# Low halves of the token projections' weights: from a negation and an accumulating DMA to one subtraction on VectorE

## The chip, the core and the metric

The kernel runs on one core of one Trainium2 chip. The metric is the device time of one execution in microseconds (us), as a median of runs; the profile is of one further execution. The engines are TensorE (PE in the profile), VectorE (DVE), ScalarE (ACT), GpSimd (POOL) and SyncE (SP).

## What is computed

One decoder layer on 512 tokens of width 1024, in float32:

```python
h = rms_norm(x, ln1_g)
z = h @ w_in                      # one input projection for all three branches and the gates
a = gelu(z_a); u, v = split(a)    # branch 0: chunked spatial gating
y_a = (u * chunked_spatial_gating(layer_norm(v), sg_w, sg_b)) @ w_a_out
c = p * sigmoid(g_lin)            # branch 1: convolution of 31 taps, layer norm, SiLU
c = silu(layer_norm(causal_depthwise_conv(c, cv_w, cv_b)))
y_b = c @ w_b_out
q, k = rms_norm(q), rms_norm(k)   # branch 2: stick-breaking attention, 8 heads of 64
y_c = stick_breaking_attention(q, k, vv) @ w_c_out
gates = sigmoid(z_g + b_gate)
x = x + (gates[0] * y_a + gates[1] * y_b + gates[2] * y_c) @ w_out
h2 = rms_norm(x, ln2_g)
up = causal_depthwise_conv(h2 @ w_up, ffn_conv_w, ffn_conv_b)   # width 3
x = x + (silu(gate) * val) @ w_down
```

## The kernel before

Every matrix product is made of three matmuls: each float32 operand is held as a high half (the value rounded to the matmul's format) and a low half (what the rounding left), and TensorE adds high times high, high times low and low times high in one PSUM bank (`mm3`, L124, L127 and L128; in the token projections L495 to L497). The activations' halves are made once. The weights come as 140 tiles of 128x1024, one after the other, and each is split on arrival by `wload`: SyncE loads the raw tile (two buffers, `wr`), ScalarE casts it to the high half `wh` (L173), and the low half `wl` follows. Six buffers hold three pairs of halves, so the halves of tile n can be written when TensorE is done with tile n-3. `wload` runs two tiles ahead of TensorE.

How the low half is made depends on the tile (`bydma`). For 120 of the tiles VectorE subtracts: raw minus high (L175; the first four tiles are split by other lines). For the 20 tiles of the token projections (the `NTOK` tiles 8 to 27: the two halves of branch 0, q, k and v) ScalarE writes minus the high half (L178) and GpSimd issues a DMA (L179) that reads the same weights from HBM once more and adds them into it.

In this text unit n is the work of TensorE on weight tile n, counted from 0: 24 matmuls of 512 columns, for full tiles. Units 0 to 7 are branch 1's input projection, 8 to 27 the token projections, then for each branch gates and outputs (branch 0: units 28 to 39, branch 1: 40 to 51 with its outputs in 44, 45, 50 and 51, branch 2: gates in 52 to 59 and outputs in 60 to 63), the output projection (64 to 71), the feed-forward's up (72 to 115) and down (116 to 139).

Between these units lies the side work of the branches, written as generators: `conv` (the 31 taps on VectorE, L363, in two pairs of channel blocks, and then the layer norm: two column sums by matmul with `onesW`, L314 and L315, the reciprocal root with ScalarE's Ln and Exp and VectorE's L320 and L134 to L136, then L397, a sigmoid on ScalarE, L402, L404 and a `split` into `cT`), `hi` (branch 0's norm and the norms of q and k), `soft` (turning q and k, L646; scores, L676 and L677; their sigmoids on ScalarE), `scan` (the cumulative products on VectorE, L723, and a multiply, L726), and `av` (turning the result, L736, splitting it, the matmuls with v, L749 and L750, into one PSUM bank whose contents L756 and L757 take out). The outputs' matmuls use two PSUM banks in turn, `mm`, which the gates' sigmoids on ScalarE or the multiply L827 on VectorE empty.

The order is a planner's. It keeps three clocks, for TensorE, VectorE and ScalarE, in modelled microseconds; `spend` moves them and `fill` lets side work be issued while the clock of the engine that it needs is behind TensorE's. Each half unit moves TensorE's clock by 2.72 (`PEU / 2`), and by `wspend` the two others by the split of the tile that is loaded next: for a tile with its low half by DMA, nothing on VectorE's clock and 1.04 on ScalarE's; for the others 0.61 and 0.52. Before a branch's outputs `finish` issues whatever is left of the side work that they need. The framework's scheduler then sets each engine's order from the order of issue, with the weights' splits, gates and evacuations first (`hot`), and every engine runs its own list in that order.

Of the kernel before, what the change touches and what calls it, by code (L numbers as in the profile page):

```python
# [11 lines left out]
AF = mybir.ActivationFunctionType  # L12
ALU = mybir.AluOpType
# [25 lines left out]
NZB, NTOK, NZG, NY, NOUT, NUP, NDN = 8, 20, 24, 12, 8, 44, 24  # L39
# [6 lines left out]
def tile_block(ctx: ExitStack, tc: tile.TileContext, xT, x0g, wall, cst, lnv, sgw, outT):  # L46
    nc = tc.nc
    act, dve, pool, pe, sp = nc.scalar, nc.vector, nc.gpsimd, nc.tensor, nc.sync
# [37 lines left out]
    f = lambda ap: ap.bitcast(F32)  # L86
# [16 lines left out]
    def load(out, in_):  # L103
        i = sp.dma_start(out=out, in_=in_)
        after(i, dlast[0])
        dlast[0] = i.ins
# [8 lines left out]
    def split(hi, lo, src):  # L115
        act.copy(out=hi, in_=src)  # L116
        dve.tensor_tensor(out=lo, in0=src, in1=f(hi), op=ALU.subtract)
# [5 lines left out]
    def mm3(out, ah, al, bh, bl, start, stop, behind=None):  # L123
        i = pe.matmul(out=out, lhsT=ah, rhs=bh, start=start, stop=False)  # L124
        after(i, behind)
        mark[0] = i.ins
        pe.matmul(out=out, lhsT=ah, rhs=bl, start=False, stop=False)  # L127
        pe.matmul(out=out, lhsT=al, rhs=bh, start=False, stop=stop)  # L128
# [9 lines left out]
    def hot():  # L138

        return tc.high_priority(int(HOT * tc.cur_priority))  # L140
# [9 lines left out]
    state = {"next": 0}  # L150
# [1 line left out]
    HOT = 0.7  # L152
    WARM = 7

    def bydma(i):

        return NZB <= i < NZB + NTOK

    def wspend():

        if bydma(state["next"]):
            spend(PEU / 2, 0, SPA)
        else:
            spend(PEU / 2, SPD / 2, SPA / 2)

    def wload(i):
        n = 768 if i >= NW - NDN and (i - (NW - NDN)) % 3 == 2 else 1024
        raw = wr.tile([P, 1024], F32, tag="wr", name="wr")
        hi = ws.tile([P, 1024], F32R, tag="w", name="wh")
        lo = ws.tile([P, 1024], F32R, tag="w", name="wl")  # L170
        load(raw[:, :n], wall[i, :, :n])
        with hot():
            act.copy(out=hi[:, :n], in_=raw[:, :n])  # L173
            if not bydma(i):
                dve.tensor_tensor(out=lo[:, :n], in0=raw[:, :n], in1=f(hi[:, :n]), op=ALU.subtract)  # L175
            else:

                act.activation(out=lo[:, :n], in_=f(hi[:, :n]), func=AF.Copy, scale=-1.0)  # L178
                pool.dma_start(out=lo[:, :n], in_=wall[i, :, :n], accum_op=ALU.add)  # L179
        wq[i] = (hi, lo)  # L180

    def wnext(i):
        while state["next"] < min(NW, i + 1 + AHEAD):
            wload(state["next"])
            state["next"] += 1
        return wq.pop(i)
# [6 lines left out]
    def spend(pe=0.0, dve=0.0, act=0.0):  # L193
        clk["pe"] += pe
        clk["dve"] += dve
        clk["act"] += act
# [14 lines left out]
    def fill():  # L211
        for k in ("dve", "act"):
            clk[k] = max(clk[k], clk["pe"] - 5.0)
        live = {n: bool(side[n]) for n in side}
        while True:
            for n, need in (("hi", ()), ("av", ()), ("scan", ()), ("conv", ("dve",)), ("soft", ("act", "dve"))):
                if live[n] and all(clk[k] < clk["pe"] for k in need):
                    live[n] = step(side[n])
                    break
            else:  # L220
                return
# [10 lines left out]
    def cd(n, s=0):  # L232
        return 0.15 + s * 0.06 + n * 0.001042
# [30 lines left out]
    for k in range(KD):  # L264
        i, j = k // 2, half[k % 2]
# [3 lines left out]
        raw, hi, lo = w4[i]  # L269
# [140 lines left out]
    def chan_unit(i, ps, xs):  # L410

        hi, lo = wnext(i)
        for k in range(KD):
            ks = slice(k * P, (k + 1) * P)
            mm3(ps, hi[:, ks], lo[:, ks], xs[k][0], xs[k][1], k == 0, k == KD - 1)
            if k == 3:
                wspend()
                fill()
        wspend()

    def group4():
        return [MM(), MM(), Z(), AV()]
# [1 line left out]
    PEU, SPD, SPA = 5.44, cd(1024), ca(1024)  # L424
# [4 lines left out]
    for kk in range(4):  # L429
        hi, lo = wnext(iw)  # L430
# [3 lines left out]
        for j in range(2):  # L434
# [6 lines left out]
            if k == 0:  # L441
# [4 lines left out]
                for c, a, b in order:  # L446
                    i = pe.matmul(out=g[c], lhsT=a[:, c * P:(c + 1) * P], rhs=xg[k][b],
                                  start=a is hi and b == 0, stop=False)
# [32 lines left out]
    def tok_group(evac, dve_c, act_c):  # L481
        nonlocal iw
        g = group4()
        for kk in range(4):
            hi, lo = wnext(iw)
            iw += 1

            order = [(c, j) for c in range(4) for j in range(2)] if kk == 3 else \
                [(c, j) for j in range(2) for c in range(4)]
            for n, (c, j) in enumerate(order):  # L490
                k = 2 * kk + j
                js = slice(j * 512, (j + 1) * 512)
                cs = slice(c * P, (c + 1) * P)
                xh, xl = xn[k][0][:, cs], xn[k][1][:, cs]
                pe.matmul(out=g[c], lhsT=xh, rhs=hi[:, js], start=k == 0, stop=False)  # L495
                pe.matmul(out=g[c], lhsT=xh, rhs=lo[:, js], start=False, stop=False)  # L496
                mark[0] = pe.matmul(out=g[c], lhsT=xl, rhs=hi[:, js], start=False, stop=k == KD - 1).ins  # L497
                if k == KD - 1:
                    with hot():
                        evac(c, g[c])  # L500
                if n == 3 or n == 7:
                    if n == 7 and kk == 3:
                        spend(0, dve_c, act_c)
                    wspend()
                    fill()


# [306 lines left out]
    def outputs(gate, src, first, last):  # L814
        nonlocal iw
        ocs = sorted(gate)
        for i2 in range(len(ocs) // 2):
            hi, lo = wnext(iw)
            iw += 1
            for jj in range(2):  # L820
                oc = ocs[2 * i2 + jj]
                ps = MM()
                for k in range(KW):
                    ks = slice((jj * KW + k) * P, (jj * KW + k + 1) * P)
                    mm3(ps, hi[:, ks], lo[:, ks], src[k][0], src[k][1], k == 0, k == KW - 1)
                with hot():
                    dve.tensor_tensor(out=gate[oc], in0=ps, in1=gate[oc], op=ALU.mult)  # L827
                if first:
                    m[oc] = gate[oc]
                else:  # L830
                    dve.tensor_tensor(out=m[oc], in0=m[oc], in1=gate[oc], op=ALU.add)
                if last:
                    mg[oc] = PR()
                    split(mg[oc][0], mg[oc][1], m[oc])
                wspend()
                spend(0, 2 * cd(T), 0)
                fill()

# [14 lines left out]
    for oc in range(KD):  # L853
        x1[oc] = S()
        sp.dma_start(out=x1[oc], in_=xT[oc])
        hi, lo = wnext(iw)
# [18 lines left out]
    for fch in range(KF):  # L875
        cv = []
        pss = []
        for gv in range(2):
            hi, lo = wnext(iw)
# [8 lines left out]
        for gv in range(2):  # L888
# [6 lines left out]
            for s in (1, 2):  # L895
                dve.scalar_tensor_tensor(out=a[:, :T - s], in0=t[:, s:T], scalar=c_("fw", ch * 3 + s),  # L896
                                         in1=a[:, :T - s], op0=ALU.mult, op1=ALU.add)
# [12 lines left out]
    for oc in range(KD):  # L910
        ps = Z()
        for k in range(KF):
            if k % 8 == 0:
                hi, lo = wnext(iw)
# [104 lines left out]
```

## Time and profile before

| | us |
|---|---|
| median of 3 runs | 804.87 (804.74 to 805.3) |
| the profiled execution's own time | 804.76 |
| its span, from the first to the last instruction | 802.9 |
| TensorE busy in the span | 796.2 |
| VectorE busy | 547.4 |
| ScalarE busy | 384.2 |

What lies around the span of the profiled execution is 804.76 - 802.9 = 1.86 us. A matmul's record overlaps with the next one's, so the busy time of TensorE says only that it is hardly ever without work; how fast it goes is read from the starts of its matmuls. DMA moved 90.96 MB at a mean of 113 GB/s, 10.49 MB of it through the queue of GpSimd's accumulating DMAs.

### The profile page before, as it was taken

The numbers are of one execution on the slowest core, as the hardware profiler recorded it, in microseconds if no ns is written. First come the engines' busy times: TensorE is split into PE (matmuls) and PEld (weight loads), VectorE is DVE, ScalarE is ACT, GpSimd is POOL, SyncE is SP. The second block draws the span as 40 slices with busy tenths as digits, with TensorE's granted clock in tenths as the row PEclk, the third lists the DMA queues.
The fourth block names the chain that finished last, engine by engine and source line by source line (L and its number), as shares of the span: only waits on it lengthen the run. The fifth ranks groups of instructions, "written<-read, shape, count | busy, mean of one in ns | idle before, by whom it ended". The sixth has DMA issues, their size and how long they took to land.

```text
span 802.9 us, 9339 instructions
## 1 busy us (share of the span) xinstructions
PE 796.2 (99%) x3607; PEld 660.4 (82%) x3607; DVE 547.4 (68%) x752; ACT 384.2 (48%) x546; POOL 44.4 (6%) x65
## 2 busy tenths in 40 slices
PE   9999999999999999999999999999999999999998
PEld 7888888887888888788888888888888888888886
DVE  7779988887797888633855777777777777322221
ACT  7476555446967486333344544444444444211110
POOL 0012111000112022000000000000000000000000
PEclk9999999999999999999999999999999999999999
DMA  7389886632231212222343322322322322333230
GB/s 270 106 226 211 186 197 153 154 106 80 80 104 57 75 53 79 78 81 104 113 140 141 105 81 103 105 92 93 105 97 87 105 104 77 109 105 134 102 105 26
DMA packets 27692, 90.96 MB, mean 113 GB/s; under 512 B 3072, under 2 KB 3712, under 8 KB 27648
## 3 DMA queue, kind: packets, MB, share of 16 engines
q1 hardware_dynamic: 24624, 79.76, 29.2%
q0 software_dynamic: 2880, 10.49, 7.8%
q8 instruction: 28, 0.46, 0.2%
q14 instruction: 16, 0.13, 0.1%
q10 hardware_dynamic: 144, 0.13, 0.0%
HBM read 88.27 MB, written 2.10 MB: 113 GB/s over the span
## 4 chain that ended last, share of the span: by engine, by line
PE 96%; ACT 1%; DVE 1%; DMA 1%; issue 0%; SPq 0%; DVEq 0%; ACTq 0%
PE z L124 18%; PE z L127 18%; PE z L128 18%; PE mm L124 8%; PE mm L128 8%; PE mm L127 8%; PE mm L496 2%; PE mm L497 2%; PE mm L495 2%; PE a L497 1%; PE z L497 1%; PE a L496 1%; PE z L496 1%; PE a L495 1%; PE z L495 1%; PE z L736 1%
## 5 line engine op out<-in xcount | busy, mean ns | idle before, releaser
L173 ACT CAST wh<-wr 128x1024 fp32r<-128x1024 f32 (+1 forms) x136 | 141.7, 1042 | 227.1 <-PE z L127 113.5
L124 PE MATMUL z<-s,wh 128*128 128x512 f32 x599 | 233.0, 389 | 0.0
L128 PE MATMUL z<-s,wl 128*128 128x512 f32 x599 | 233.0, 389 | 0.0
L127 PE MATMUL z<-s,wh 128*128 128x512 f32 x599 | 233.0, 389 | 0.0
L175 DVE TENSOR_TENSOR wl<-wr,wh 128x1024 fp32r<-128x1024 f32 (+1 forms) x116 | 140.2, 1209 | 107.9 <-ACT wh L173 106.5
L128 PEld LDWEIGHTS z<-s,wl 128*128 128x128 f32 x599 | 112.4, 188 | 23.4
L124 PEld LDWEIGHTS z<-s,wh 128*128 128x128 f32 x599 | 112.4, 188 | 23.4
L127 PEld LDWEIGHTS z<-s,wh 128*128 128x128 f32 x599 | 112.4, 188 | 23.3
L124 PE MATMUL mm<-s,wh 128*128 128x512 f32 x302 | 120.4, 399 | 0.5 <-ACT s L113 0.4
L127 PE MATMUL mm<-s,wh 128*128 128x512 f32 x302 | 117.6, 389 | 0.0
L128 PE MATMUL mm<-s,wl 128*128 128x512 f32 x302 | 117.3, 391 | 0.0
L363 DVE SCALAR_TENSOR_TENSOR s<-s,cst 128x511 f32<-128x511 f32 (+29 forms) x120 | 80.2, 732 | 0.0
L128 PEld LDWEIGHTS mm<-s,wl 128*128 128x128 f32 x302 | 56.7, 188 | 12.4
L896 DVE SCALAR_TENSOR_TENSOR h<-h,cst 128x511 f32<-128x511 f32 x88 | 65.7, 748 | 1.5
L124 PEld LDWEIGHTS mm<-s,wh 128*128 128x128 f32 x302 | 56.8, 188 | 12.1 <-ACT s L113 1.0
L127 PEld LDWEIGHTS mm<-s,wh 128*128 128x128 f32 x302 | 56.8, 188 | 10.7
L893 DVE TENSOR_TENSOR h<-z,rs 128x512 f32<-128x512 f32 x44 | 30.2, 687 | 39.8 <-PE z L128 39.8
L894 ACT ACTIVATE h<-h,cst 128x512 f32<-128x512 f32 x44 | 35.9, 816 | 3.2 <-DVE h L893 3.0
L116 ACT CAST s<-h 128x512 fp32r<-128x512 f32 x18 | 11.2, 620 | 49.1 <-DVE h L901 49.1
L113 ACT ACTIVATE h<-h 128x512 f32<-128x512 f32 x22 | 13.9, 632 | 41.9 <-DVE h L896 41.9
L495 PE MATMUL mm<-wh,s 128*128 128x512 f32 x80 | 31.2, 390 | 0.0
L496 PE MATMUL mm<-wl,s 128*128 128x512 f32 x80 | 31.1, 389 | 0.0
(184 smaller groups left out, 901.0 us busy)
## 6 DMA issues: line engine op xcount, KB each, us to landing
wr<-wall SPq DMA_DIRECT2D x128, 512.0 KB, 3.3
wl<-wall POOLq DMA_DIRECT2D x20, 512.0 KB, 5.5
s<-xT SPq DMA_DIRECT2D x15, 256.0 KB, 4.1
wr<-wall SPq DMA_DIRECT2D x8, 384.0 KB, 3.1
outT<-s SPq DMA_DIRECT2D x7, 256.0 KB, 2.0
h<-wall SPq DMA_DIRECT2D x3, 512.0 KB, 6.9
s<-sgw SPq DMA_DIRECT2D x2, 256.0 KB, 4.3
s<-lnv SPq DMA_DIRECT2D x2, 256.0 KB, 5.5
```

The costliest lines, as they stand in the source:

```text
L124: i = pe.matmul(out=out, lhsT=ah, rhs=bh, start=start, stop=False)
L127: pe.matmul(out=out, lhsT=ah, rhs=bl, start=False, stop=False)
L128: pe.matmul(out=out, lhsT=al, rhs=bh, start=False, stop=stop)
L173: act.copy(out=hi[:, :n], in_=raw[:, :n])
L175: dve.tensor_tensor(out=lo[:, :n], in0=raw[:, :n], in1=f(hi[:, :n]), op=ALU.subtract)
L363: after(dve.scalar_tensor_tensor(out=acc[j][:, :T - s], in0=cc[j][:, s:], scalar=c_("cvw", j * TAPS + s), in1=acc[j][:, :T - s], op0=ALU.m ...
L495: pe.matmul(out=g[c], lhsT=xh, rhs=hi[:, js], start=k == 0, stop=False)
L496: pe.matmul(out=g[c], lhsT=xh, rhs=lo[:, js], start=False, stop=False)
L497: mark[0] = pe.matmul(out=g[c], lhsT=xl, rhs=hi[:, js], start=False, stop=k == KD - 1).ins
L893: dve.tensor_tensor(out=t[:, :T], in0=pss[gv], in1=rs2, op=ALU.mult)
L894: act.activation(out=a, in_=t[:, :T], func=AF.Identity, scale=c_("fw", ch * 3), bias=c_("fb", ch))
L896: dve.scalar_tensor_tensor(out=a[:, :T - s], in0=t[:, s:T], scalar=c_("fw", ch * 3 + s), in1=a[:, :T - s], op0=ALU.mult, op1=ALU.add)
```

## The change

All tiles are split in the one way: `wload` calls `split`, which casts on ScalarE (now L116) and subtracts on VectorE (now L117). `bydma` is gone, and with it `wspend`: each half unit now moves the planner's clocks by the same amounts for all tiles, so for each of the 20 tiles VectorE's clock moves by 1.22 more and ScalarE's by 1.04 less than before. In the changed file all later lines have numbers that are smaller by 17 (L363 is L346, L827 is L810, and so on).

```diff
--- before.py
+++ after.py
@@ -152,17 +152,6 @@
     HOT = 0.7
     WARM = 7
 
-    def bydma(i):
-
-        return NZB <= i < NZB + NTOK
-
-    def wspend():
-
-        if bydma(state["next"]):
-            spend(PEU / 2, 0, SPA)
-        else:
-            spend(PEU / 2, SPD / 2, SPA / 2)
-
     def wload(i):
         n = 768 if i >= NW - NDN and (i - (NW - NDN)) % 3 == 2 else 1024
         raw = wr.tile([P, 1024], F32, tag="wr", name="wr")
@@ -170,13 +159,7 @@
         lo = ws.tile([P, 1024], F32R, tag="w", name="wl")
         load(raw[:, :n], wall[i, :, :n])
         with hot():
-            act.copy(out=hi[:, :n], in_=raw[:, :n])
-            if not bydma(i):
-                dve.tensor_tensor(out=lo[:, :n], in0=raw[:, :n], in1=f(hi[:, :n]), op=ALU.subtract)
-            else:
-
-                act.activation(out=lo[:, :n], in_=f(hi[:, :n]), func=AF.Copy, scale=-1.0)
-                pool.dma_start(out=lo[:, :n], in_=wall[i, :, :n], accum_op=ALU.add)
+            split(hi[:, :n], lo[:, :n], raw[:, :n])
         wq[i] = (hi, lo)
 
     def wnext(i):
@@ -414,9 +397,9 @@
             ks = slice(k * P, (k + 1) * P)
             mm3(ps, hi[:, ks], lo[:, ks], xs[k][0], xs[k][1], k == 0, k == KD - 1)
             if k == 3:
-                wspend()
+                spend(PEU / 2, SPD / 2, SPA / 2)
                 fill()
-        wspend()
+        spend(PEU / 2, SPD / 2, SPA / 2)
 
     def group4():
         return [MM(), MM(), Z(), AV()]
@@ -501,7 +484,7 @@
                 if n == 3 or n == 7:
                     if n == 7 and kk == 3:
                         spend(0, dve_c, act_c)
-                    wspend()
+                    spend(PEU / 2, SPD / 2, SPA / 2)
                     fill()
 
 
@@ -832,7 +815,7 @@
                 if last:
                     mg[oc] = PR()
                     split(mg[oc][0], mg[oc][1], m[oc])
-                wspend()
+                spend(PEU / 2, SPD / 2, SPA / 2)
                 spend(0, 2 * cd(T), 0)
                 fill()
```

The planner and the scheduler make another order of this. On VectorE, in the token projections: before, the taps of the convolution (`s<-s,cst`) and branch 0's norm stand there without a weight's split between them.

```order
L117 TENSOR_TENSOR s<-s 128x512
L535 BN_AGGR mv<-st 128x2
L534 BN_STATS st<-b 128x6 x2
L535 BN_AGGR mv<-st 128x2
L363 SCALAR_TENSOR_TENSOR s<-s,cst 128x495
L535 BN_AGGR mv<-st 128x2
L534 BN_STATS st<-b 128x6
```

With the change the same norm's statistics stand seven taps of each channel block earlier (after the first tap of 503 columns, not after the last of 496), and a low half stands after every 2 to 13 instructions:

```order
L518 BN_AGGR mv<-st 128x2
L529 SCALAR_TENSOR_TENSOR b<-b,mv,s 128x512
L346 SCALAR_TENSOR_TENSOR s<-s,cst 128x501 x2
L346 SCALAR_TENSOR_TENSOR s<-s,cst 128x500
L523 TENSOR_SCALAR v_890<-mv 128x4
L529 SCALAR_TENSOR_TENSOR b<-b,mv,s 128x512
L346 SCALAR_TENSOR_TENSOR s<-s,cst 128x500
L117 TENSOR_TENSOR wl<-wr,wh 128x1024
L346 SCALAR_TENSOR_TENSOR s<-s,cst 128x499 x2
```

So the taps as a whole have moved to later units. On TensorE the first 31 units are in the same order as before; after them the side work has moved. The layer norm's column sums stood in units 31 and 34 and now stand in 39 and 42; head 0's scores in unit 34, now behind unit 43; the last attention matmul in unit 54, now in unit 60. Where branch 1's outputs begin (unit 44, banks `mm_2148` and `mm_2163`; `s_2084`, `s_2091`, `s_2117` and the numbers one above are the high and low halves of `cT`) TensorE now has this, with nothing else of the units between it and the second column sum but the rest of unit 42 and unit 43:

```order
L660 MATMUL z_2192<-s_1879,s_1877 128x128
L629 MATMUL z_2203<-ident_204,s_1012 128x128
L629 MATMUL z_2203<-ident_204,s_1020 128x128
L124 MATMUL mm_2148<-s_2084,wh_2033 128x512
L629 MATMUL z_2203<-ident_204,s_1031 128x128
...
L127 MATMUL mm_2148<-s_2085,wh_2033 128x512
L128 MATMUL mm_2148<-s_2084,wl_2034 128x512
L124 MATMUL mm_2148<-s_2091,wh_2033 128x512
L127 MATMUL mm_2148<-s_2092,wh_2033 128x512
```

Between the second matmul of that column sum and this first output stand 46 matmuls; in the order of before 294 stand between them. On VectorE the end of that norm now stands like this (`s_2085`, `s_2092`, `s_2118` and `s_2139` are the four low halves of `cT`; `h_2179` is head 0's scan, `wl_2144` the low half of unit 46, and L810 empties the bank of unit 44's first product):

```order
L387 TENSOR_TENSOR s_575<-s_575,s_1933 128x512
L117 TENSOR_TENSOR wl_2144<-wr_2142,wh_2143 128x1024
L117 TENSOR_TENSOR s_2085<-s_575,s_2084 128x512
...
L117 TENSOR_TENSOR s_2118<-s_1284,s_2117 128x512
L385 TENSOR_SCALAR s_1286<-s_1286,cst_85 128x512
L387 TENSOR_TENSOR s_1286<-s_1286,s_1991 128x512
L706 SCALAR_TENSOR_TENSOR h_2179<-h_2179,s_862 128x512
L117 TENSOR_TENSOR s_2139<-s_1286,s_2138 128x512
L706 SCALAR_TENSOR_TENSOR h_2179<-h_2179,s_862 128x384
L706 SCALAR_TENSOR_TENSOR h_2179<-h_2179,s_862 128x256
L810 TENSOR_TENSOR s_1988<-mm_2148,s_1988 128x512
```

Before, the same norm's end stood among branch 0's outputs, and its last low half, too, had other work around it:

```order
L402 TENSOR_SCALAR s_980<-s_980,cst_85 128x512
L117 TENSOR_TENSOR s_2047<-s_978,s_2046 128x512
L757 TENSOR_TENSOR s_2072<-a_2008,s_2072 64x512
L404 TENSOR_TENSOR s_980<-s_980,s_1744 128x512
L827 TENSOR_TENSOR s_1922<-mm_2082,s_1922 128x512
L175 TENSOR_TENSOR wl_2098<-wr_2096,wh_2097 128x1024
L117 TENSOR_TENSOR s_2079<-s_980,s_2078 128x512
L827 TENSOR_TENSOR s_1973<-mm_2102,s_1973 128x512
```

## Rows read from the trace of the kernel before

**Rows 1.** The page: engines' busy time, share of the span, instructions; granted clock by slices.

```profile
span 802.9 us, 9339 instructions
...
PE 796.2 (99%) x3607; PEld 660.4 (82%) x3607; DVE 547.4 (68%) x752; ACT 384.2 (48%) x546; POOL 44.4 (6%) x65
...
PEclk9999999999999999999999999999999999999999
```

**Rows 2.** Busy time by stretches, whole core.

```profile
core 0: us, PE busy (x) PEld busy (x) DVE busy (x) ACT busy (x) POOL busy (x), PEclk, DMA share, GB/s
...
60.00:80.00 20.00, 20.00 (x90) 16.57 (x89) 20.00 (x34) 13.13 (x16) 4.78 (x6) 1.00 0.92 210
```

**Rows 3.** Waits, TensorE alone: who waited for whom, total, times, longest.

```profile
PE z L247 <- POOL ident masks.py:197: 1.3, 1, 1.3
...
PE mm L124 <- ACT s L113: 0.4, 1, 0.4
```

**Rows 4.** Timeline of TensorE, first gates of branch 0: start, length.

```profile
163.26 0.39 PE L124 MATMUL mm<-s,wh 128*128 128x512 f32 x1
...
168.71 0.39 PE L124 MATMUL mm<-s,wh 128*128 128x512 f32 x1
```

**Rows 5.** Groups by form, VectorE.

```profile
L175 DVE TENSOR_TENSOR wl<-wr,wh 128x1024 fp32r<-128x1024 f32 x108 | 132.6, 1227 | 107.9 <-ACT wh L173 106.5
...
L723 DVE TENSOR_TENSOR_SCAN h<-h,s 128x512 f32<-128x512 f32 x8 | 9.9, 1236 | 4.6 <-ACT h L113 4.3
...
L402 DVE TENSOR_SCALAR s<-s,cst 128x512 f32<-128x512 f32 x4 | 2.2, 541 | 0.1
```

**Rows 6.** Groups by form, ScalarE.

```profile
L173 ACT CAST wh<-wr 128x1024 fp32r<-128x1024 f32 x128 | 134.9, 1054 | 205.0 <-PE z L127 91.4 <-PE a L496 40.9 <-PE mm L127 36.1
...
L178 ACT ACTIVATE wl<-wh 128x1024 fp32r<-128x1024 f32 x20 | 21.2, 1059 | 0.3
...
L113 ACT ACTIVATE s<-s 128x512 f32<-128x512 f32 x8 | 5.0, 629 | 7.7 <-DVE s L320 4.5 <-DVE s L348 3.2
...
L113 ACT ACTIVATE s<-s,cst 128x512 f32<-128x512 f32 x4 | 3.2, 830 | 0.0
```

**Rows 7.** DMA issues: size, median us from issue to landing.

```profile
wl<-wall POOLq DMA_DIRECT2D x20, 512.0 KB, 5.5
```

**Rows 8.** Timeline of VectorE, second norm of the convolution branch.

```profile
217.07 0.69 DVE L136 SCALAR_TENSOR_TENSOR s<-s 128x512 f32<-128x512 f32 x1
217.79 1.29 DVE L397 TENSOR_TENSOR s<-s 128x512 f32<-128x512 f32 x2
...
220.67 1.22 DVE L175 TENSOR_TENSOR wl<-wr,wh 128x1024 fp32r<-128x1024 f32 x1
221.80 0.42 DVE L117 TENSOR_TENSOR s<-z,s 128x256 fp32r<-128x256 f32 x1
...
231.69 0.67 DVE L404 TENSOR_TENSOR s<-s 128x512 f32<-128x512 f32 x1
```

**Rows 9.** Timeline of TensorE: that norm's sum, last attention matmul, branch 2's outputs.

```profile
205.83 0.40 PE L315 MATMUL z<-s,onesW 128*128 128x512 f32 x1
...
265.98 0.52 PE L736 MATMUL z<-ident,h 128*128 128x128 f32 x3
266.25 0.47 PE L124 MATMUL mm<-s,wh 128*128 128x512 f32 x1
...
344.04 0.28 PE L750 MATMUL a<-s,b 128*128 128x128 f32 x1
...
374.14 0.39 PE L124 MATMUL mm<-s,wh 128*128 128x512 f32 x1
```

**Rows 10.** Timeline of TensorE at its longest wait in the middle.

```profile
325.40 0.39 PE L128 MATMUL mm<-s,wl 128*128 128x512 f32 x1
326.77 0.47 PE L749 MATMUL a<-s,b 128*128 128x512 f32 x1 [0.98 <-DVE s L757]
```

**Rows 11.** Groups, TensorE: the seven warm-up matmuls.

```profile
L247 PE MATMUL z<-s 128*128 128x512 f32 x7 | 3.3, 651 | 1.3 <-POOL ident masks.py:197 1.3
```

## The prediction

> **What bounds the kernel now.** I read the page first. TensorE is busy 796.2 of 802.9 us, and the granted clock reads nine tenths or more in every slice [rows 1]. Then the stretches: in 60 to 80 us VectorE is busy all 20.00 us and DMA shows its highest share, 0.92, and TensorE still makes 90 matmuls at a granted clock of 1.00, its 2.4 GHz level [rows 2]. Then the pace. Unit 28 starts at 163.26 and unit 29 at 168.71 [rows 4]: 24 matmuls in 5.45 us, 0.227 us each. So the time of this kernel is the number of matmuls times 0.227 us plus the waits of TensorE, and the waits are small: 1.3 us at the start, 0.4 for a gate [rows 3], and one of 326.77 - 325.40 - 0.23 = 1.14 us where a matmul waits for VectorE to empty the attention's bank [rows 10]. The change leaves the matmuls as they are. It can win at most the last two, about 1.5 us, and it loses whatever new waits it makes for TensorE. A load on another engine costs nothing until TensorE stands still for it, and so I look for places where it would.
>
> **What the change removes.** Twenty negations on ScalarE at 1.059 us, 21.2 us [rows 6], and twenty transfers of 512 KB, each 5.5 us from issue to landing [rows 7]. TensorE waits for none of them in the trace, so their removal is worth 0. Their cover is the two units by which weights are split ahead.
>
> **What it adds.** Twenty subtractions at 1.227 us [rows 5], 24.5 us on VectorE. Are they in time? A pair of buffers comes free two units, 10.9 us, ahead of its use. The cast takes 1.05 [rows 6] and the subtraction 1.23; that leaves 8.6 us for VectorE to come round to it. Between two low halves stand at most 13 other instructions, and most take a step of about 0.61 to 0.66 us (two multiplies that follow each other take 1.29, the second's own 0.68 off gives a step of 0.61 [rows 8]), 8.5 us at the very most and mostly 4 to 6. Added up row by row from the first token unit, each low half is done 7 to 10 us before TensorE comes to it. I take 0; if that cover were gone, each late low half would cost up to its own 1.23. The raw tile is now held until the subtraction, one instruction longer, within a unit of 5.45: 0.
>
> **What it moves.** The planner now counts 1.22 us more of VectorE per token tile, so the taps are spread thinner and end later, and all that hangs on them too. In the trace the second column sum of the convolution's norm starts at 205.83 and the first outputs of branch 1 at 266.25, 60 us later; the last attention matmul is at 344.04 and branch 2's outputs start at 374.14, 30 us later [rows 9]. In the new order 46 matmuls and nothing else stand between that column sum and branch 1's outputs, and the last attention matmuls stand within branch 2's first output unit. Both reserves are used up. What is late there is added up next.
>
> **Term A, unit 44.** Let 0 be the end of the column sum. TensorE reaches unit 44 after 36 matmuls of 0.227, eight scores of together 2560 columns (1.13 at the same pace) and two turns of 0.09 (three take 0.27 before 266.25 [rows 9]), less 0.17 by which a matmul's record, 0.40, outlasts its step: 9.3 us. The norm meanwhile: VectorE's L320 at about 0.7 to 0.74; Ln and Exp at 0.63 [rows 6] to 2.05; three steps of 0.72 [rows 8] to 4.25; the low half of unit 45, a step of 1.13 [rows 8], to 5.4; four multiplies at 0.61 to 7.85; two scale-and-shifts (0.54 alone [rows 5], about 0.5 as a step) and a multiply to 9.45; the low half of unit 46, for which ScalarE first ends three sigmoids of 0.83 [rows 6] at 8.6 and then casts, to 10.8; the first low half of `cT` at 11.4; the second and third, after a multiply, a scale-and-shift and a multiply, by 14.4. For the fourth, ScalarE has a gate's sigmoid and then the last of the four, to 15.3; a scale-and-shift and a multiply end at 16.4; then stands a scan of head 0, 1.24 alone [rows 5] and 1.14 as a step, to 17.8, and then the last low half, 18.4. TensorE waits there for each half in turn. It has four matmuls left behind the last and ends unit 44 at 19.3. Without waits it would be 9.3 + 5.45 + six turns of 0.09 = 15.3: **4.0 us lost**. And unit 45 needs the bank of unit 44's first product, which VectorE empties behind two more scans (0.9 and 0.6 by their columns) and a step of 0.65, at 20.6: **1.3 us more**. A is 5.3. From below: if VectorE took nothing in between but the norm, the sum would be about 13.6, ahead of need, and A would be 0. From above: before, the same norm took from 206.23 to 231.69 + 0.67 [rows 8, 9], 26.1 us, with other work in between; with cast and low half 27.4 and 0.9 of matmuls behind them, A would be 28.3 - 15.3 = 13. I take the worked sum, since the order names each instruction that stands between.
>
> **The other terms.** In unit 47 the turns of head 0 come behind its multiply L726, which in the same sum ends about 0.5 us late: **0.5**. The wait for the attention's bank, 1.14 in the trace [rows 10], I count once again, as TensorE meets the same pair (L749 behind L757) at the end of unit 51: **1.1**. In unit 60 the last head's chain is: two casts, a table load, a cast, a copy, two casts and a copy on ScalarE, the add, the cast and the low half; against 11 matmuls, eight of attention and seven more it is late by **0.9**. Sum: 5.3 + 0.5 + 1.1 + 0.9 = 7.8, less the 1.5 of old waits, is +6.3. With the profiled execution's own 804.76 that is **811.1 us**, 0.8% over it; the median of the runs, 804.87, is 0.11 above that execution, so I forecast 811.1 for the median too.
>
> **Rivals.** The measurement tells about 0.2%, 1.6 us, from nothing.
>
> *No change.* VectorE runs the norm tighter than I sum it, A is near its lower end, and the last head is not late. For it speaks that the scheduler put these rows where it thought them ready, and that in all of 802.9 us the order of before left TensorE 1.5 us of such waits. Against it speaks that `finish` has issued the rest of the norm in one go, with no units in between. The time: 803.3 to 806.5. It decides when the last low half of `cT` comes before 14.4 on the scale above, so that four matmuls end by 15.3. The Trainium skill's "Perfetto Trace Analysis" (Identifying the Most-Contended Engine) would have it this way: gains come from the engine with the highest occupancy, and VectorE at 68% is not that one; by it the time stays at 804.9. The trace agrees that TensorE is that engine [rows 1]. Chance 0.11.
>
> *Faster.* The old waits go and none come: 803.3. Chance 0.03.
>
> *Lows late in the token units.* In 60 to 80 us VectorE has no idle time [rows 2]. If the taps don't make way, half of the twenty subtractions, 12 us, come out as waits there: 804.8 + 12 + A or so, 818 to 824. Against it speaks the sum above. Chance 0.07.
>
> *The clock.* If TensorE's waits of together 4 us in unit 44 made the granted clock fall to its 1.2 GHz level, the matmuls behind them would take longer: the seven at the very start, after a stretch without work, show 651 ns [rows 11] against 390 later [rows 4], 0.26 us more. For two units at two places that is 96 times 0.26, 25 us: 836. Against it: through the 1.14 us wait at 325 the clock stays in the top tenth [rows 1, 10], and the waits of unit 44 are single ones of about 1 us between matmuls. The Trainium skill's "TensorE: Matmul & The Clock Gate" (Part 1) says that an idle engine is put back to the half clock; no run here shows such a fall yet. Chance 0.04.
>
> **How the numbers follow.** The forecast, waits at units 44 to 60 of 2.5 to 12 us net, has 0.75. Slower by over 0.2% is 0.75 + 0.07 + 0.04 = 0.86; within it 0.11; faster 0.03. The range is 806 to 817: the lower end leaves out the faster case and most of the unchanged one, the upper end the clock, most of the late lows and the upper end of A; together some 2 in 10.
>
> **What would show it.** In the changed kernel: TensorE steps of 5.45 us a unit with no wait up to unit 43; in unit 44 waits of 0.5 to 1 us for the halves of `cT` (L124 and L127 behind ScalarE's L116 and VectorE's L117), about 4 us together, and one of 1 us or more before unit 45 behind L810; single waits under 1.2 us in the attention; the granted clock in the top tenth throughout; and from the up projection on the same stretch as before. Wrong would be: waits of TensorE for weights (`wl`) before unit 42, a norm that ends before TensorE comes, or waits in units 45 to 60 that add up to more than unit 44's.

## The result, and the profile after

The changed kernel takes **814.79 us** (median of 4 runs, 813.7 to 815.07), the kernel before 804.89 beside it (804.74 to 805.3): ratio 1.0119, 95% interval 1.0108 to 1.0131. That is 1.2% slower. The forecast was slower, 811.1 us; the range of 806 to 817 holds the result. The profiled execution is the fastest of the four, 813.7 us with a span of 811.5 and a mean granted clock of 1.000; the other three have spans of 812.5 to 812.9 at 0.997 to 0.998.

The page after, busy time of the engines and the two lines of slices that answer to [rows 1]:

```profile
PE 799.0 (98%) x3607; PEld 659.8 (81%) x3607; DVE 571.0 (70%) x772; ACT 365.2 (45%) x526; POOL 25.8 (3%) x45
...
PE   9999999999998999989999999999999999999998
...
PEclk9999999999999999999999999999999999999999
```

The work went where the change sends it: VectorE 547.4 to 571.0 us, ScalarE 384.2 to 365.2, and the traffic fell from 90.96 MB to 80.46. TensorE has the same 3607 matmuls and a span that is 8.6 us longer; two slices (the 13th and the 18th) now read 8. Its waits of 0.9 us and more together (engine, matmul, what ended the wait, total, times, longest), answer to [rows 3]:

```profile
PE z L659 <- DVE s L117: 2.2, 1, 2.2
PE z L230 <- POOL ident masks.py:197: 1.3, 1, 1.3
PE mm L124 <- DVE s L810: 1.3, 2, 1.0
PE mm L124 <- ACT s L116: 1.2, 3, 0.5
PE a L732 <- DVE s L740: 1.2, 2, 0.9
PE mm L127 <- DVE s L117: 0.9, 2, 0.6
```

The third, fourth and sixth lines are for the most part unit 44 and the bank before unit 45, as predicted (the rest of the third and fourth is in and behind unit 60); the fifth is the attention's bank; the first was not predicted. Unit 44 on TensorE (start, duration, instruction; in brackets the idle time and what ended it):

```profile
253.44 0.27 PE L660 MATMUL z<-s 128*128 128x128 f32 x1
...
254.31 0.50 PE L124 MATMUL mm<-s,wh 128*128 128x512 f32 x1 [0.36 <-ACT s L116]
...
256.66 0.51 PE L124 MATMUL mm<-s,wh 128*128 128x512 f32 x1 [0.52 <-ACT s L116]
257.80 0.50 PE L127 MATMUL mm<-s,wh 128*128 128x512 f32 x1 [0.63 <-DVE s L117]
...
264.50 0.50 PE L124 MATMUL mm<-s,wh 128*128 128x512 f32 x1 [1.00 <-DVE s L810]
```

From the last score matmul at 253.44 to unit 45 at 264.50 are 11.06 us. The work between is a step of 0.06, eight turns of 0.09 and 24 matmuls of 0.227: 6.23. So **4.8 us** are lost here, the predicted term A of 5.3. The column sum, the last low half of `cT` and the emptied bank, on TensorE and VectorE:

```profile
243.92 0.40 PE L298 MATMUL z<-s,onesW 128*128 128x512 f32 x1
```

```profile
261.55 0.71 DVE L117 TENSOR_TENSOR s<-s 128x512 fp32r<-128x512 f32 x1
...
263.79 1.26 DVE L810 TENSOR_TENSOR s<-mm,s 128x512 f32<-128x512 f32 x2
```

From the end of the column sum at 244.32, the low half is done after 17.9 us (18.4 in the prediction), and unit 45 starts after 20.2 (20.6).

The wait that was not predicted lies in unit 55. VectorE there, and then TensorE:

```profile
342.50 3.12 DVE L706 TENSOR_TENSOR_SCAN h<-h,s 128x512 f32<-128x512 f32 x4 [0.52 <-ACT h L113]
345.72 1.49 DVE L709 TENSOR_TENSOR h<-h 128x1279 f32<-128x1279 f32 x1
347.25 1.16 DVE L117 TENSOR_TENSOR s<-z,s 128x512 fp32r<-128x512 f32 x2
```

```profile
345.40 0.40 PE L660 MATMUL z<-s 128*128 128x512 f32 x1
347.99 0.44 PE L659 MATMUL z<-s 128*128 128x384 f32 x1 [2.20 <-DVE s L117]
```

The five PSUM banks `z` go round. The score matmul at 347.99 wants the bank in which TensorE had put a turned attention block at 341.3; VectorE may split that block only behind the four scans and the multiply of the next head, and ends the split at about 347.9. The step from 345.40 to 347.99 is 2.59, less 0.23: 2.4 us.

### The profile page after: what moved, and what is told of

Same layout as the page of the kernel before. It is cut to its first block, busy times and chain, and to the rows that moved or that the text cites. A ratio compares the mean times of both kernels' runs of the same rounds, so it can differ in the third digit from the quotient of the medians.

```text
span 811.5 us, 9287 instructions
## 1 busy us (share of the span) xinstructions
PE 799.0 (98%) x3607; PEld 659.8 (81%) x3607; DVE 571.0 (70%) x772; ACT 365.2 (45%) x526; POOL 25.8 (3%) x45
## 2 busy tenths in 40 slices
DMA packets 24810, 80.46 MB, mean 99 GB/s; under 512 B 2752, under 2 KB 3392, under 8 KB 24768
## 4 chain that ended last, share of the span: by engine, by line
PE 91%; DVE 5%; ACT 3%; issue 1%; DMA 1%; SPq 0%; DVEq 0%; ACTq 0%
PE z L128 18%; PE z L124 18%; PE z L127 18%; PE mm L124 7%; PE mm L127 7%; PE mm L128 7%; PE mm L478 2%; PE mm L479 2%; PE mm L480 2%; DVE h L706 1%; PE a L478 1%; PE z L478 1%; PE a L479 1%; PE z L479 1%; PE a L480 1%; PE z L480 1%
## 5 line engine op out<-in xcount | busy, mean ns | idle before, releaser
L116 ACT CAST wh<-wr 128x1024 fp32r<-128x1024 f32 (+1 forms) x136 | 141.8, 1042 | 241.6 <-PE z L127 113.0
L117 DVE TENSOR_TENSOR wl<-wr,wh 128x1024 fp32r<-128x1024 f32 (+1 forms) x136 | 164.8, 1211 | 92.9 <-ACT wh L116 91.0
L346 DVE SCALAR_TENSOR_TENSOR s<-s,cst 128x511 f32<-128x511 f32 (+29 forms) x120 | 81.1, 731 | 0.0
L124 PEld LDWEIGHTS mm<-s,wh 128*128 128x128 f32 x302 | 56.6, 188 | 16.4 <-ACT s L116 2.8
L116 ACT CAST s<-h 128x512 fp32r<-128x512 f32 x18 | 11.2, 620 | 49.1 <-DVE h L884 49.1
L669 POOL TENSOR_SCALAR_AFFINE_SELECT h<-h 128x128 f32<-128x128 f32 x32 | 21.7, 688 | 316.8 <-ACT h L113 316.7
L113 ACT ACTIVATE h<-z,qs 128x512 f32<-128x512 f32 (+3 forms) x64 | 28.4, 556 | 6.3 <-PE z L660 6.3
```

The lines of the kernel that those rows point to most:

```text
L113: chained(act.activation(**kw))
L346: after(dve.scalar_tensor_tensor(out=acc[j][:, :T - s], in0=cc[j][:, s:], scalar=c_("cvw", j * TAPS + s), in1=acc[j][:, :T - s], op0=ALU.m ...
```

## The experiments

There are two things in the change, work (twenty subtractions for twenty negations and transfers) and order (the planner counts the subtractions). The theory ahead of the runs: the order alone costs the time. Its rival: the work does. All ratios are to runs of the kernel before on the same chip, of 804.5 to 804.9 us in the median.

**Work alone.** All low halves by subtraction, the planner's accounts as before.

```diff
-            if not bydma(i):
-                dve.tensor_tensor(out=lo[:, :n], in0=raw[:, :n], in1=f(hi[:, :n]), op=ALU.subtract)
-            else:
-                act.activation(out=lo[:, :n], in_=f(hi[:, :n]), func=AF.Copy, scale=-1.0)
-                pool.dma_start(out=lo[:, :n], in_=wall[i, :, :n], accum_op=ALU.add)
+            split(hi[:, :n], lo[:, :n], raw[:, :n])
```

> The new work in the old order: all low halves by VectorE's subtraction, but the planner's clocks are moved as before the change (nothing on VectorE's for the 20 token tiles). Theory (the order makes the loss, VectorE has room for the work): the column sums are back in units 31 and 34, the last attention matmul in unit 54, and the time is that of before, 803.5 to 806.5 us. Rival (VectorE is overloaded by the 24.5 us): 811 us or more, with TensorE waiting for VectorE in the token units or later.

Measured: 812.42 us, ratio 1.0096 (1.0081 to 1.0111). The theory missed. Units 44 to 60 have no waits beyond those of before, but behind unit 19 there is a new one. TensorE, and the engines by stretches (busy time, number of instructions, granted clock, DMA share, GB/s):

```profile
114.71 0.39 PE L491 MATMUL a<-wh,s 128*128 128x512 f32 x1
119.24 0.91 PE L124 MATMUL z<-s 128*128 128x256 f32 x2 [4.15 <-ACT s L116]
```

```profile
50.00:110.00 60.00, 60.00 (x267) 49.67 (x266) 59.89 (x93) 24.48 (x32) 0.00 (x0) 1.00 0.31 106
...
116.00:119.00 3.00, 0.00 (x0) 0.00 (x0) 3.00 (x5) 0.43 (x1) 0.00 (x0) 1.00 0.03 12
...
120.50:124.00 3.50, 3.48 (x16) 3.36 (x17) 3.50 (x6) 2.19 (x5) 0.00 (x0) 0.54 0.01 4
124.00:126.00 2.00, 2.00 (x14) 1.75 (x13) 2.00 (x4) 0.00 (x0) 0.00 (x0) 1.00 0.00 0
```

The third busy column is VectorE: 59.89 of 60 us. The matmuls of branch 0's spatial gating wait for its norm, which on VectorE stands mixed with taps:

```profile
116.66 1.22 DVE L117 TENSOR_TENSOR wl<-wr,wh 128x1024 fp32r<-128x1024 f32 x1
117.79 0.74 DVE L542 SCALAR_TENSOR_TENSOR b<-b,y,s 128x512 f32<-128x512 f32 x1
118.46 1.40 DVE L357 SCALAR_TENSOR_TENSOR s<-s,cst 128x510 f32<-128x510 f32 x2
119.78 0.68 DVE L117 TENSOR_TENSOR s<-b,s 128x512 fp32r<-128x512 f32 x1
```

The subtraction at 116.66 has a step of 1.13 (the next starts at 117.79), so twenty take 22.6 us. How much room was there? VectorE before, by stretches:

```profile
50.00:110.00 60.00, 57.34 (x97) 1.00 0.88 202
110.00:163.00 53.00, 45.15 (x81) 1.00 0.71 165
163.00:200.00 37.00, 30.78 (x43) 1.00 0.25 87
```

From 50 us on it was idle for 2.7 + 7.8 + 6.2 = 16.7 us up to 200, where the convolution's norm is due in that order, and for only 2.7 before 110. So the work does not fit into the old order, and the rival was right for it.

**Order alone.** The negation and the DMA stay, the planner counts as in the change.

```diff
-        if bydma(state["next"]):
-            spend(PEU / 2, 0, SPA)
-        else:
-            spend(PEU / 2, SPD / 2, SPA / 2)
+        spend(PEU / 2, SPD / 2, SPA / 2)
```

> The old work in the new order: the 20 low halves by negation and accumulating DMA, but the planner's clocks are moved as after the change. Theory (the order alone makes the loss): 812.5 to 816 us, with the same waits of TensorE in units 44, 45, 51, 55 and 60, although VectorE has 24.5 us less to do. Rival (the subtractions make it): 805 us, or well under 811.

Measured: 813.88 us (813.07 to 815.14), ratio 1.0115 (1.01 to 1.013). Without one subtraction more than before, the order takes the change's time: the two medians differ by 0.9 us, and the ranges overlap. Its waits are the change's:

```profile
PE z L673 <- DVE s L117: 2.2, 1, 2.2
...
PE mm L124 <- DVE s L824: 1.3, 2, 1.0
PE mm L124 <- ACT s L116: 1.3, 3, 0.5
```

So either part alone loses, 7.8 and 9.3 us, and both together 9.9: the order of the change pays for room that the work needs, and pays more than the room is worth.

**The dose.** As the first run, but only every second token tile by subtraction.

```diff
-            if not bydma(i):
+            if not (bydma(i) and i % 2):
```

> The kernel before, with ten of its twenty token tiles (every second) split by subtraction and ten still by negation and accumulating DMA; accounts of before. Theory (VectorE had 10.5 us without work between 50 and 163 us, 12.5 - 8 of it before unit 19 is reached; twenty subtractions are 23 us of steps, six of twelve before unit 19 about 7 us less than in the run with all twenty): the 4.3 us wait of unit 19 is gone, 804.5 to 806.5. Rival (each subtraction costs its share of the 7.8 us): 808.5.

(The idle time that this text puts before unit 19 is muddled: by the stretches above it is 2.7 us before 110.) Measured: 805.29 us, ratio 1.0007 (0.9998 to 1.0016). Ten subtractions, 11.3 us, fit into the 16.7, twenty don't. VectorE by the first stretch, and the one new wait of TensorE, which is 0.6 us by its steps:

```profile
50.00:110.00 60.00, 59.97 (x97) 1.00 0.61 156
```

```profile
PE z L127 <- DVE s L117: 0.4, 1, 0.4
```

A share per subtraction would have cost 3.9 us; measured are 0.5. So the loss is no share per subtraction, and fits what overflows.

**Norm of branch 0 first.** The first run again, with that norm ahead of the taps.

```diff
-            split(vn[h][0], vn[h][1], va[:, :, h * P:(h + 1) * P])
+            with hot():
+                split(vn[h][0], vn[h][1], va[:, :, h * P:(h + 1) * P])
```

(and the same `with hot()` around the root of its statistics and its two scalings)

> The planner's accounts of before (subtractions not counted for the token tiles), all low halves by subtraction, and branch 0's norm (its statistics' root, the two scalings, its splits) issued ahead of the taps. Theory: the 4.3 us wait in unit 19 came from taps standing ahead of that norm on a VectorE that was full; with the norm first it is gone, the taps end later but still ahead of unit 44's need, and TensorE keeps the three waits of before (0.5, 0.3, 1.1): 804 to 806, no difference from before. Rival (VectorE has 12 us too much to do in the token units, wherever it stands): the wait comes out elsewhere, at q's or k's norm, at the convolution's norm or in unit 44, and the time stays at 809 or above.

Measured: 810.7 us, ratio 1.0071 (1.0058 to 1.0083). The wait of unit 19 is gone, as the theory has it, but others stand at and in unit 32, as the rival has it: 1.7 us for a gate's bank (0.5 before), and 1.6 and 0.9 around the first column sum, for which the taps now come late. VectorE around them:

```profile
182.42 5.15 DVE L357 SCALAR_TENSOR_TENSOR s<-s,cst 128x485 f32<-128x485 f32 x8
...
191.44 0.69 DVE L117 TENSOR_TENSOR s<-s 128x512 fp32r<-128x512 f32 x1 [0.68 <-ACT s L116]
```

What overflows moves to the next piece of work with a due time. By the stretches before, 22.6 - 16.7 = 5.9 us should overflow up to 200. The new waits come to less, 3.8 us: 0.3 behind unit 21, the 1.6 and the 0.9, and the 1.1 by which the gate's bank is later, and that bank waits for ScalarE, whose sigmoid stands behind a cast of weights. The span grew by 5.6 all the same (808.5 against 802.9): behind these waits the granted clock fell, and eight matmuls took steps of about 0.43 us and not 0.23, which is 1.6 us more (last section).

**The change with the norm of branch 1 a unit earlier.**

```diff
+            if b == 1:
+                finish(*need)
```

(ahead of the gates' units, and not behind them)

> The changed kernel with the rest of the convolution's norm issued ahead of branch 1's gates instead of behind the first four of them; its second column sum moves from unit 42 to unit 41. Theory (unit 44 is late by the norm's chain of about 19 us): with one more unit, 5.45 us, the waits of units 44 and 45, together 4.6 us, fall under 1; the attention is as late as it was, so the time is 809.5 to 811.5. Rival (the waits of unit 44 go elsewhere, to the new place of the column sum): 813 to 815.

Measured: 819.42 us, ratio 1.0181 (1.0164 to 1.0198). Both expectations missed. Units 44 and 45 wait no longer, but a matmul of unit 42 waits 9.28 us for its bank. ScalarE's list shows why: the sigmoid that empties it stands behind the whole norm's chain.

```profile
251.88 0.62 ACT L116 CAST s<-s 128x512 fp32r<-128x512 f32 x1 [1.65 <-DVE s L387]
252.52 1.27 ACT L113 ACTIVATE s<-mm,cst 128x512 f32<-128x512 f32 x2
```

Issued sooner, the chain (here from the table load before 244 to the last cast at 251.88) is no shorter, and an order must have other work for TensorE meanwhile.

**The change with the turned blocks split first.**

```diff
-            split(ah[:, :n], al[:, :n], pt[:, :n])
+            with hot():
+                split(ah[:, :n], al[:, :n], pt[:, :n])
```

> The changed kernel with the splits of the turned attention blocks put first in the scheduler's choice, so that in unit 55 the split that frees a bank stands two instructions earlier on VectorE (ahead of the 128-column scan and the 1279-column multiply, steps of 0.54 and 1.5 us). Theory (the 2.4 us wait of unit 55 is that bank, held up by VectorE's order): that wait falls to about 0.3, and the time by about 2 us, to 812.5; if the granted clock in runs at 0.997 or 0.998 fell behind that wait, it reads 0.999 or more here and the time falls by 3, to 811.8. Rival (the wait is for something else, the scores' sources): no change, 814.8.

Measured: 811.52 us (811.39 to 812.02), ratio 1.0085 (1.007 to 1.01). The same score matmul, which now starts 0.50 us behind the one before it and has no idle time that the profile notes:

```profile
345.88 0.44 PE L659 MATMUL z<-s 128*128 128x384 f32 x1
```

The wait of unit 55 falls from 2.4 to 0.3, all others stay; the span falls from 811.5 to 809.4, the median by 3.3 (by 3.0 if each median is set against its own runs of before). All four runs have a granted clock of 0.999 or 1.000.

**Cheaper account of VectorE in the changed kernel**, so that taps are issued earlier, and the same with both pieces of the last runs first (`hot()` around branch 0's norm and the turned blocks' splits).

```diff
-        return 0.15 + s * 0.06 + n * 0.001042
+        return 0.08 + s * 0.04 + n * 0.001042
```

> The changed kernel with one number of the planner altered: an instruction on VectorE counts 0.08 + 0.04 per operand and not 0.15 + 0.06, nearer to what it takes in the trace. The convolution's column sums move from units 38 and 42 to 33 and 35, the last attention matmuls from unit 60 to 54. Theory (the order alone costs the time, VectorE can do the work): the waits of units 44, 45 and 60 and the late split of unit 55 are gone, 804 to 807. Rival (VectorE overcommitted, as with the accounts of before): branch 0's norm comes late in unit 19 by some us, 809 to 813.

> The cheaper account, and both branch 0's norm and the splits of the turned attention blocks issued first. Theory: as the run with the cheaper account alone or up to 2.5 less, where that has a wait in unit 19 or behind the scans; 803.5 to 805.5. Rival: what is put first makes the taps late, and waits of 1 us or more come back in unit 44: 806 to 810.

Measured: 810.03 us, ratio 1.0064 (1.005 to 1.0078), and 808.6, ratio 1.0045 (1.0032 to 1.0058). Units 19, 44 and 60 wait for nothing, nor does unit 45 for its bank, so what the theory said of those holds, but its times don't. The times lie in the rivals' ranges, but not for the rivals' reasons: the attention, a gate and a bank of the outputs wait at places of which neither had spoken. Of the second the longest, by TensorE's steps, is 1.7 us, a turn of the attention behind VectorE's L646, and five more are of 0.3 to 1.0, while before has three of 0.3 to 1.1.

**A third of the subtractions counted** (35%, accounts between those of before and of the change), with three pieces first: the two of the last run and what empties the attention's bank.

```diff
-            spend(PEU / 2, 0, SPA)
+            spend(PEU / 2, SPD * 0.175, SPA / 2)
```

> All low halves by subtraction on VectorE, 35% of each of the token tiles' subtractions counted by the planner, and three pieces issued first: branch 0's norm, the splits of the turned attention blocks, and what empties the attention's bank. The column sums stand in units 35 and 37, the last attention matmuls in unit 57. Theory (an order that leaves VectorE some 12 us more before the convolution's norm than that of before, and the norm more than that of the change, has room for the subtractions): the waits of units 19, 31, 44, 45, 51, 55 and 60 are all small, 803.5 to 806.5, the best with all twenty on VectorE. Rival (every order with these 23 us on VectorE collides somewhere): waits of 1 us or more at the attention's turns or scores, 807 to 811.

Measured: 810.76 us, ratio 1.008 (1.0066 to 1.0094): the rival. Two waits of 1.9 us, in unit 43 and before unit 48 (a turn behind VectorE's L657, and a bank behind a sigmoid on ScalarE), and six of 0.3 to 1.0.

**GpSimd instead of VectorE.** The kernel before, accounts and all, with the twenty subtractions on GpSimd, which is nearly idle.

```diff
-                act.activation(out=lo[:, :n], in_=f(hi[:, :n]), func=AF.Copy, scale=-1.0)
-                pool.dma_start(out=lo[:, :n], in_=wall[i, :, :n], accum_op=ALU.add)
+                pool.tensor_tensor(out=lo[:, :n], in0=raw[:, :n], in1=f(hi[:, :n]), op=ALU.subtract)
```

> The kernel before, with the negation and the accumulating DMA of the twenty token tiles replaced by a subtraction on GpSimd; accounts of before, nothing added on VectorE. Theory (the removal of negation and DMA is worth nothing, and all of the loss is VectorE's time and what the planner makes of it): TensorE keeps the three waits of before, 804 to 806. Rival (the two engines get in each other's way, or GpSimd is too late): VectorE's steps get longer while GpSimd works, unit 19 waits again, 808 or above.

Measured: 830.46 us, ratio 1.0316 (1.0298 to 1.0333): the rival, and worse. Two pieces of the timeline, GpSimd's and VectorE's:

```profile
57.27 2.50 POOL L178 TENSOR_TENSOR wl<-wr,wh 128x1024 fp32r<-128x1024 f32 x1 [3.62 <-ACT wh L173]
...
107.69 9.64 POOL L178 TENSOR_TENSOR wl<-wr,wh 128x1024 fp32r<-128x1024 f32 x1 [10.54 <-ACT wh L173]
```

```profile
57.44 2.89 DVE L362 SCALAR_TENSOR_TENSOR s<-s,cst 128x510 f32<-128x510 f32 x1
60.25 0.68 DVE L351 TENSOR_TENSOR s<-z,s 128x512 f32<-128x512 f32 x1
...
115.05 2.30 DVE L134 SCALAR_TENSOR_TENSOR smt<-y,v 128x4 f32<-128x4 f32 x1
```

A tap takes 0.74 otherwise. The one at 57.44 takes 2.89: it ends 0.56 after GpSimd's subtraction, which ends at 59.77. And GpSimd's subtraction at 107.69 takes 9.64, while VectorE runs about a dozen instructions, nearly all taps, without a gap (one more takes 8.0, the other eighteen 2.4 to 3.6); TensorE waits 7.1 us for that low half, its longest wait in this run. Then it is VectorE's turn to wait: L134, on 4 columns and 0.16 us otherwise, takes 2.30 from 115.05 on and ends with GpSimd's subtraction, which ends at 117.33. So the two engines exclude each other here. The Trainium skill's "SBUF — State Buffer" (Who interferes with whom) says that an instruction of VectorE with two SBUF inputs contends with one of GpSimd that reads SBUF, and that the loser is blocked for the other's whole instruction; VectorE's two long rows agree, and GpSimd's long one shows it held up for many instructions in a row.

**The bank of the attention first**, in the run with branch 0's norm first and in the kernel before, unchanged otherwise.

```diff
-                act.copy(out=o32[r], in_=av[(1 - h % 2) * HD:(2 - h % 2) * HD])
-                dve.tensor_tensor(out=o32[r], in0=av[r], in1=o32[r], op=ALU.add)
+                with hot():
+                    act.copy(out=o32[r], in_=av[(1 - h % 2) * HD:(2 - h % 2) * HD])
+                    dve.tensor_tensor(out=o32[r], in0=av[r], in1=o32[r], op=ALU.add)
```

> The run with the accounts of before and branch 0's norm first, and besides the copy and the add that empty the attention's bank issued first. Theory: the one wait of 1.1 us that the kernel before has behind its full bank goes too, 803.0 to 804.2 if the norm's run equals before: 0.1 to 0.2% faster than before. Rival: the add comes no earlier, since it waits for ScalarE's copy; no gain over that run.

> The kernel before, with only the copy and the add that empty the attention's bank issued first. Theory (TensorE's waits are all that there is to win): the wait of 1.14 us in unit 51 goes, 803.5 to 804.1. Rival: it comes back at another place as the scans are pushed behind, 804.6 to 805.2.

Measured: 809.7 us, ratio 1.0056 (1.0043 to 1.0068), 1.0 us less than that run (its expected time rested on that run being at 804 to 806), and 803.52 us, ratio 0.9986 (0.9977 to 0.9995). The second is faster than the kernel before by 0.14%, and so than the changed one too. In both the 1.1 us wait of unit 51 is gone. What the second is left with:

```profile
PE z L247 <- POOL ident masks.py:197: 1.3, 1, 1.3
PE mm L124 <- ACT s L113: 0.4, 1, 0.4
```

## Why the prediction was right, and where it was off

- **The mechanism held**: the loss is TensorE's waits, made by the later order, with the norm of branch 1 as the largest. The run with the order alone shows it with the work of before. (That the time is the number of matmuls times 0.227 holds for those of 512 columns only: 3607 times 0.227 would be 819 us.)
- **Removal worth 0**: consistent with every run. In the run with the order alone negation and DMA are there, and the two kernels' runs overlap (813.07 to 815.14 and 813.7 to 815.07); half of them gone at the old order changes 0.07%, within its interval.
- **Subtractions worth 0**: true of the weights themselves, since no matmul waits for a `wl` in the changed kernel. But it was read in the new order alone. In the old order they cost 7.8 us, not as late lows but through what they push back, the norm of branch 0. The prediction had no rival for that.
- **Term A, 5.3**: measured 4.8, 3.7 of it in unit 44 (predicted 4.0) and 1.2 at the bank (1.3). A list of steps, each from a row, came within a tenth, and at its points along the way within 0.6 us. One step in it is added up wrong: a scan of 1.14 from 16.4 on ends at 17.5 and not 17.8; with that A would have been 5.0.
- **Unit 47, 0.5; unit 51, 1.1; unit 60, 0.9**: 0.4, 1.1 and 1.5. In unit 60 there were three waits of 0.4 to 0.5 where I summed one chain.
- **Unit 55, not in the sum**: 2.4 us, the step that failed. I followed operands and the banks `a` and `mm`, and not the round of the five banks `z`. With that split first the span falls by 2.1.
- **Net**: the terms as measured, 4.8 + 0.4 + 1.1 + 1.5 + 2.4 = 10.2, less the old waits, are 8.2 of the 8.6 us by which the span grew; predicted was 6.3. The old waits are 2.0 by the same steps (0.5, 0.3 and 1.1) where I had 1.5. The median came out 3.7 above the forecast, and unit 55 is the largest part of that; the range was wide enough to hold it.
- **The signs**: one of those that the prediction called wrong did come. The waits of units 47 to 60 add up to 5.4 us (6.6 with the bank before unit 45), more than the 3.7 of unit 44, and one wait in the attention is 2.4 where single ones under 1.2 were expected. So the cause, the later order, was right, and the share of the norm in the loss was put too high: A is 4.8 of the 8.2, where it was 5.3 of 6.3. The others held: no wait for a `wl`, no norm that ends before TensorE comes.
- **From the profiled execution to the median**: I set them equal. The median is 1.1 us above the profiled execution, at a clock of 0.997 to 0.998 against 1.000. In the run with the turned blocks first the clock stays at 0.999 or above, and the median falls by about 1 us more than the span of the profiled execution (3.3 against 2.1). That it is the 2.4 us wait which lowers the clock in some executions is argued from this, not shown; the changed kernel has no profile of such an execution. The run with branch 0's norm first has one, at 0.998, with a single fall (last section), and its two executions at 0.999 and 1.000 have spans of 807.8 and 807.7 where the other three have 808.5 to 808.8.
- **The clock rival, 836**: it didn't come; the profiled execution reads 1.000, and what the three others lost is the 1 us or so above. Where a fall was seen, behind other waits, it cost 1.2 to 2.2 us by TensorE's steps and not the 25 that I priced, since the clock was soon back at 1.00 (below). A step there is 0.43, 0.20 more than 0.23, and not 0.26 more.

Open: whether an order with all twenty subtractions on VectorE can do without the loss. Of the eight that were run beside the changed kernel's own the best is 0.45% behind the kernel before.

## What to carry to other kernels

An engine at 68% mean busy can be nearly full where it counts (57.34 of 60 us here): add up its idle time to the next due piece of work, and compare the added work with that (here 22.6 us against 16.7 cost 7.8, and 11.3 cost 0.5, within the noise). What overflows tells that there will be a loss, not how large it is. Where a planner or scheduler counts the work, run the work and the count apart, since each alone can cost as much as both. And follow each late instruction to all that it holds: its result, its PSUM bank in the round, and its engine's list behind it.

## What the runs showed of the hardware that was not expected

The granted clock fell after waits of a few us. Behind the 4.15 us wait of unit 19 it is 0.54 for 3.5 us and 1.00 again from 124 on; that costs an estimated 1.6 us (3.5 times 0.46) of the 7.8 that the work alone lost. Behind the wait of 9.28 us, by stretches of TensorE alone:

```profile
246.00:253.00 7.00, 0.00 (x0) 0.60 0.08 31
253.00:257.00 4.00, 3.74 (x9) 0.50 0.01 4
257.00:258.00 1.00, 1.00 (x5) 0.65 0.00 0
258.00:260.00 2.00, 2.00 (x11) 1.00 0.00 0
```

It fell to half, the 1.2 GHz level, during the wait, the first matmuls behind it, from 253.26 on, ran at that level, and from 258 on it is 1.00 again. A single long wait is not needed. In the run with branch 0's norm first TensorE waited 1.66, 1.56 and 0.89 us by its steps, before 187.58, 191.56 and 193.44, with 14 matmuls between the first and the last, and then the clock fell:

```profile
187.50:193.90 6.40, 4.21 (x16) 0.99 0.25 82
193.90:197.20 3.30, 3.30 (x10) 0.51 0.00 0
197.20:199.00 1.80, 1.80 (x9) 1.00 0.04 9
```

The same run with the attention's bank first has the same waits and the same fall. In the changed kernel's profiled execution the four waits of unit 44 and the one for the bank behind it, 0.3 to 1.0 us each with work between them, and the one of 2.2 us in unit 55 left the clock at 1.00. The Trainium skill's "TensorE: Matmul & The Clock Gate" (Part 1), that an idle engine is put back to the half clock, is borne out by the first two cases; the kernel before shows such a fall only behind its last matmul (0.52 from 801.6 us on), where it costs nothing. And where VectorE and GpSimd block each other the kernel took 25.7 us more, with a single subtraction of GpSimd drawn out from 2.4 to 9.64 us; three falls of the clock are part of that.
